# Moving the cached log-forget values into the first adaLN groups, and the decay chain into the first q tile, in a fused decode-step kernel

## The chip, the cores and the metric

The kernel runs on one core of one Trainium2 chip. The metric is device microseconds (us) of one execution of the whole program; lower is better. The kernel before took 1068.47 us (median of 3 runs, 1067.93 to 1070.03). The execution that was profiled took 1067.71 us; its trace spans 1066.1 us from the first to the last instruction, so 1.6 us lie around it. A core has five instruction queues that run side by side, each strictly in its own order: PE (matmul; its weight loads are listed as PEld), DVE (vector), ACT (scalar, activation functions and casts), POOL (GpSimd) and SP (used here only to issue DMAs). They wait for one another through semaphores.

## What is computed

One layer of a decoder trunk, in float32, for 512 prompt tokens and 8 single-token samples that share all weights (so 520 columns of activations), with D = 1024, 16 heads of 64, FFN width 2816:

```
m = silu(c) @ ada_w + ada_b      -> shift1, scale1, gate1, shift2, scale2, gate2
h = rms_norm(x) * (1 + scale1) + shift1
z = h @ w_in   -> rg_x | rg_gate | q | k | v | forget logits | gate A | gate B
branch A: width-4 causal conv -> RG-LRU -> * gelu(rg_gate) -> @ w_proj_a
branch B: forgetting attention, logit[t,s] = q_t.k_s/sqrt(dh) + sum_{s<j<=t} log f_j
          (samples attend to 1024 cached rows each, found through page_table)
x = x + gate1 * ((sigmoid(gA)*A + sigmoid(gB)*B) @ w_o)
x = x + gate2 * SwiGLU(rms_norm(x) * (1 + scale2) + shift2);  final rms_norm
```

For the samples, the sum of log f over the cached rows behind each row is needed: `cache_logf` is gathered by the page table (64 pages of 128 rows x 16 heads), and for every row the values after it are summed. RG-LRU needs `-8 * softplus(-lambda)` per channel (the decay), and the convolution needs, for the samples, the sum over the three stored inputs times their filter taps.

## The kernel before, in words

Activations lie feature-major: 8 tiles of 128 features x 520 tokens, worked on as two halves of 260. Every large product is made of three float32r products (high x high, low x high, high x low): each weight unit of 128 columns arrives by DMA (`wraw`, a ring of two 1 MB buffers), ACT casts its high part (`whi`, L210), DVE subtracts for the low part (`wlo`, L211), and PE runs 48 matmuls on it (`half_product`, L245). `begin` asks for weight chunks 22 us and for splits 11 us of PE time ahead. Evacuations are ACT's or DVE's.

**Start.** SP loads the parameters (L91), the constants up to column C_TRI (L92), x (L99) and the page table (L364, L366). ACT squares x, DVE adds, PE sums over features with an all-ones matmul (`ss`, L483, after feature tile 3 and after tile 7). Then `first_mod(0, ...)` (L410) runs the first half of adaLN's shift1 and scale1: eight groups `adaf` (L416), each behind its own 512 KB `araw` load (L413). ACT takes the two square roots (L488), DVE the reciprocals (L489) and eight products `xn` (L492). `first_mod_end` (L420) copies, transposes and adds, giving `n1amp`; `q_weights` (L449) splits the first q weights; `first_h` (L436) makes h for four feature tiles and PE starts the partial q products (`qp`, L467). The second half of adaLN is spread among these.

**q tiles.** A loop over i = 0..7 (L829 on) finishes q. In its turns stand: at i = 4 `past_load()` (POOL gathers 64 rows of 8 KB of log f, L371, into a buffer of the `wraw` ring) and the forget logits; at i = 6 their close, `decay()` (L599: Abs, Exp and a log1p of some twenty tiny DVE instructions on 128x8) and `past_conv()` (L807: eight products and a sum on DVE), and `past_turn(0)` (L380); at i = 7 `past_turn(1)`. `past_turn` transposes eight 64x128 blocks on PE into a bank (`lft`, L383), ACT copies it (`lk`, L385), and POOL makes the running sums over the pages behind (`after`: a memset, a copy and six dependent adds, L389 to L392). From i = 5 on, `tick` starts the sample attention: POOL loads cached key pages (L622) into a ring of seven 512 KB buffers (`pg`) that adaLN's `araw` tiles share, and DVE multiplies and sums them (L663/L664), which is what frees those buffers.

**First tiles of branch A.** The loop over i = 0, 2, 4, 6 (L980 on) runs two convolution products (`xr`), gate A (`ga`) and the RG-LRU gates (`gate`, L915, which need the split convolution `xch`/`xcl`, L278/L279), then gate B (`gb`) twice. `past_sums(0)` and `past_sums(1)` (L395) stand after the first and second `gb`: two 512-column float32 matmuls (`suf`, L398 and L399) and an ACT copy each. Then `ada_load(1, 6)` asks for the next adaLN weights (L296), the next `xr` runs, and `ada_piece(1, 6)` (L308) uses them. `suf` is first read by the softmax over the cached keys (L704).

**What sets the order.** The framework orders each engine's instructions by its own cost estimates; `with tc.issue_after(ins)` ties an instruction behind another of the same engine. `state["mm"]`, `state["act"]`, `state["last"]` hold the last tied PE, ACT and DVE instruction.

Of the kernel before, what the change touches and what calls it, by code (L numbers as in the profile page):

```python
# [64 lines left out]
def kernel(ctx, tc, xT, par, gates, b_f, cst, cse, own, cache_k, cache_v, cache_lf, pt,  # L65
# [13 lines left out]
    def slot(name, cols=NT, dt=F32, parts=128):  # L79
        return heap.tile([parts, cols], dt, name=name, tag="slot")  # L80
# [284 lines left out]
    idx = keep.tile([NS * NPAGE, 1], I32, name="idx")  # L365
    sp.dma_start(idx, pt.rearrange("a (b c) -> (a b) c", c=1))  # L366
    lfp = []

    def past_load():
# [10 lines left out]
    def past_turn(b):  # L380
        tp = bank(f"lft{b}")
        for n in range(8):
            pe.transpose(tp[:, 64 * n:64 * n + 64], lfp[0][:, 8 * b + n], ident[:64, :64])  # L383
        lk = slot("lk", 512)
        act.copy(lk, tp)  # L385
        after = slot("after", 512)
        lkv = lk.rearrange("p (a j) -> p j a", j=NPAGE)
        lav = after.rearrange("p (a j) -> p j a", j=NPAGE)
        pool.memset(lav[:, 7], 0.0)  # L389
        pool.tensor_copy(lav[:, 6], lkv[:, 7])  # L390
        for j in range(5, -1, -1):
            pool.tensor_tensor(lav[:, j], lav[:, j + 1], lkv[:, j + 1], ALU.add)  # L392
        lks.append((lk, after))

    def past_sums(b):  # L395
        lk, after = lks[b]
        sf = bank(f"suf{b}")
        pe.matmul(sf, lhsT=cs[:, C_TRI:C_TRI + 128], rhs=lk, start=True, stop=False)  # L398
        pe.matmul(sf, lhsT=ones, rhs=after, start=False, stop=True)  # L399
        t = slot("suf", 512)  # L400
        act.copy(t, sf)
        suf.append(t)


# [5 lines left out]
    def first_mod(fh, acc, kqs):  # L410
        for kq in kqs:
            raw = pgp.tile([128, 2, 512], F32, name="araw", tag="pg")
            sp.dma_start(raw, ada_w[kq * 128:kq * 128 + 128, :2048].rearrange("p (v c) -> p v c", v=2)  # L413
                         [:, :, 512 * fh:512 * fh + 512])
            for g in range(4):
                pe.matmul(acc[32 * g:32 * g + 32, :256], lhsT=silc[:, kq],  # L416
                          rhs=raw[:, g // 2, 256 * (g % 2):256 * (g % 2) + 256],
                          start=kq == 0, stop=kq == KT - 1, tile_position=(0, 32 * g))

    def first_mod_end(fh, acc):  # L420
        sb = slot("adas", 256)
        act.copy(sb, acc[:, :256])
        tp = bank(f"adaft{fh}")
        for b in range(2):
            pe.transpose(tp[:, b * 128:b * 128 + 128], sb[:, b * 128:b * 128 + 128], ident)
# [7 lines left out]
        dve.scalar_tensor_tensor(amp1[:, fs], mod[:, 1, fs], 1.0, prm[:, fs, P_N1:P_N1 + 1].to_broadcast([128, 4, 9]),  # L433
                                 ALU.add, ALU.mult)

    def first_h(f):  # L436
        t, hi, lo = slot("hr"), slot("hh", dt=F32R), slot("hl", dt=F32R)
        a_, b_ = amp1[:, f, 0:1], mod[:, 0, f, 0:1]
        act.activation(hi[:, :NP], xn[f][:, :NP], AF.Identity, scale=a_, bias=b_)
# [3 lines left out]
        act.copy(hi[:, NP:], t[:, NP:])  # L443
        dve.tensor_tensor(lo, t, hi.bitcast(F32), ALU.subtract)
        h.append((hi, lo))

# [2 lines left out]
    def q_weights(fh, raw, ko, i):  # L449
# [4 lines left out]
        src = raw[:, ko:ko + 4]  # L454
        for k in range(0, 4, 2 if (fh, i) == (0, 0) else 4):
            ks = slice(k, k + 2 if (fh, i) == (0, 0) else 4)
            state["act"] = act.copy(hi[:, ks], src[:, ks])
            state["last"] = dve.tensor_tensor(lo[:, ks], src[:, ks], hi[:, ks].bitcast(F32), ALU.subtract)
# [11 lines left out]
    def wraw():  # L470
        return wp.tile([128, KT, 256], F32, name="wraw", tag="wraw", bufs=2)

    ssq = [bank(f"ss1_{j}") for j in range(2)]
    for f in range(KT):
        t = slot("sq1")
        act.activation(t, x[f], AF.Square)
        if f % 4:
            dve.tensor_tensor(sq, sq, t, ALU.add)
        else:
            sq = t  # L480
        if f % 4 == 3:
            for j, (t0, t1) in enumerate(HALVES):
                pe.matmul(ssq[j][:, :HALF], lhsT=ones, rhs=sq[:, t0:t1], start=f == 3, stop=f == KT - 1)  # L483
    acc = [bank(f"adaf{fh}") for fh in range(2)]
    first_mod(0, acc[0], range(KT))
    r1 = slot("r1")
    for j, (t0, t1) in enumerate(HALVES):
        act.activation(r1[:, t0:t1], ssq[j][:, :HALF], AF.Sqrt, bias=eps, scale=1.0 / D)  # L488
        dve.reciprocal(r1[:, t0:t1], r1[:, t0:t1])  # L489
    for f in range(KT):  # L490
        t = slot("xn")
        dve.tensor_tensor(t, x[f], r1, ALU.mult)  # L492
# [29 lines left out]
    raw = wraw()  # L522
    q_weights(1, raw, 0, 4)
    load_chunks(0)
    sp.dma_start(cs[:, C_TRI:], cst[:, C_TRI:])


    def log1p(name, e, n, out):
# [300 lines left out]
    for i in range(KT):  # L829
# [150 lines left out]
    for i in range(0, KT, 2):  # L980
# [19 lines left out]
        if i < 6:  # L1000
# [586 lines left out]
```

## Time and profile before

| | us |
|---|---|
| median of 3 runs | 1068.47 |
| profiled execution | 1067.71 |
| its span | 1066.1 |
| PE busy | 1021.3 (96%) |
| DVE busy | 664.0 (62%) |
| ACT busy | 494.2 (46%) |
| POOL busy | 202.2 (19%) |

Timeline rows have: start, duration, engine, source line, operation, output<-inputs, how many were merged, and in brackets how long the engine had been idle before and what ended that wait. Rows of the windows view have: the stretch, its length, then for each engine the busy time and number of instructions, the granted PE clock (1.00 is full), the DMA engines' busy share, and GB/s. Rows of the waits view have: who waited, for whom, total us, times, longest us. "SPq" is the queue that issues DMAs; landing times are not in its durations.

### The profile page before, as it was taken

How to read it: one execution, taken by the hardware profiler on the slowest of the kernel's cores; microseconds unless marked ns; L12 is line 12 of the kernel's file. 1: busy time of each engine (PE TensorE's matmuls, PEld its weight loads, DVE VectorE, ACT ScalarE, POOL GpSimd, SP SyncE). 2: the span in 40 equal slices, each digit the busy share in tenths (PEclk: the TensorE clock that was granted, in tenths of full speed). 3: DMA queues.
4: the chain of work that ended last, by engine and by line, in shares of the span. 5: the costliest groups of instructions: out<-in, count | busy, mean ns of one | idle time of the engine just before them, and what ended most of it. 6: DMA issues, size and time to landing. Idle time of an engine off the chain costs nothing.

```text
span 1066.1 us, 21006 instructions
## 1 busy us (share of the span) xinstructions
PE 1021.3 (96%) x8210; PEld 948.1 (89%) x8210; DVE 664.0 (62%) x1166; ACT 494.2 (46%) x976; POOL 202.2 (19%) x348
## 2 busy tenths in 40 slices
PE   4999899999999999999999999999999999999994
PEld 2888779999998987888898989999999999999993
DVE  5447999988999986656765447733343333443363
ACT  4423565757782367767783235523212232123251
POOL 0224511112134234544400014100000000000022
PEclk9999899999999999999999999999999999999998
DMA  9898887778788998987746852232333332332212
GB/s 327 281 320 286 279 297 208 260 240 297 255 283 280 351 314 263 259 252 250 248 172 216 313 166 70 73 88 79 109 90 80 97 102 80 95 104 80 72 55 74
DMA packets 165285, 206.95 MB, mean 194 GB/s; under 512 B 9778, under 2 KB 126018, under 8 KB 165122
## 3 DMA queue, kind: packets, MB, share of 16 engines
q1 hardware_dynamic: 147746, 149.90, 45.6%
q0 software_dynamic: 13760, 49.29, 13.6%
q10 hardware_dynamic: 3680, 6.42, 1.6%
q8 instruction: 64, 1.05, 0.4%
q14 instruction: 35, 0.29, 0.1%
HBM read 192.49 MB, written 13.09 MB: 193 GB/s over the span
## 4 chain that ended last, share of the span: by engine, by line
PE 76%; DVE 9%; issue 4%; DMA 4%; ACT 4%; POOL 2%; POOLq 1%; SPq 0%; ACTq 0%; DVEq 0%
PE fiu L245 11%; PE fig L245 11%; PE fo L245 9%; PE pb L245 4%; PE k L245 4%; PE v L245 4%; PE pa L245 3%; PE gr L245 3%; PE gb L245 3%; PE ga L245 3%; PE xr L245 3%; PE wo L245 3%; PE pv L751 3%; DMA wraw<-in_w_in_dram 2%; PE qp L467 2%
## 5 line engine op out<-in xcount | busy, mean ns | idle before, releaser
L211 DVE TENSOR_TENSOR wlo<-wraw,whi 128x1024 fp32r<-128x1024 f32 (+1 forms) x131 | 160.7, 1227 | 159.3 <-ACT whi L210 153.2
L210 ACT CAST whi<-wraw 128x1024 fp32r<-128x1024 f32 (+1 forms) x131 | 136.7, 1043 | 242.7 <-PE fo L245 74.6
L337 POOL TENSOR_TENSOR ss<-ss,sq 128x260 f32<-128x260 f32 x18 | 13.6, 756 | 419.5 <-ACT sq L336 419.0
L245 PE MATMUL fiu<-h2h,wlo 128*128 128x260 f32 x320 | 90.5, 283 | 0.0
L245 PE MATMUL fig<-h2h,wlo 128*128 128x260 f32 x320 | 90.5, 283 | 0.0
L245 PE MATMUL fig<-h2l,whi 128*128 128x260 f32 x320 | 90.2, 282 | 0.0
L245 PE MATMUL fiu<-h2l,whi 128*128 128x260 f32 x320 | 90.2, 282 | 0.0
L245 PE MATMUL fig<-h2h,whi 128*128 128x260 f32 x320 | 90.2, 282 | 0.0
L245 PE MATMUL fiu<-h2h,whi 128*128 128x260 f32 x320 | 90.2, 282 | 0.0
L245 PE MATMUL fo<-ach,whi 128*128 128x260 f32 x292 | 82.8, 284 | 0.0
L245 PE MATMUL fo<-ach,wlo 128*128 128x260 f32 x292 | 82.5, 282 | 0.0
L245 PE MATMUL fo<-acl,whi 128*128 128x260 f32 x292 | 82.3, 282 | 0.0
L622 POOL DMA_DIRECT2D pg<-in_cache_k_dram x79 | 42.1, 533 | 115.8 <-DVE S L668 61.1
L245 PEld LDWEIGHTS fiu<-h2h,whi 128*128 128x128 f32 x320 | 60.2, 188 | 0.0
L245 PEld LDWEIGHTS fig<-h2h,whi 128*128 128x128 f32 x320 | 60.2, 188 | 0.0
L245 PEld LDWEIGHTS fig<-h2l,whi 128*128 128x128 f32 x320 | 60.2, 188 | 0.0
L245 PEld LDWEIGHTS fiu<-h2l,whi 128*128 128x128 f32 x320 | 60.2, 188 | 0.0
L245 PEld LDWEIGHTS fig<-h2h,wlo 128*128 128x128 f32 x320 | 60.1, 188 | 0.0
L245 PEld LDWEIGHTS fiu<-h2h,wlo 128*128 128x128 f32 x320 | 60.1, 188 | 0.0
L667 DVE TENSOR_TENSOR pg<-pg,qb 128x1024 f32<-128x1024 f32 x48 | 57.4, 1213 | 1.1 <-DMA pg<-in_cache_k_dram 1.0
L668 DVE TENSOR_REDUCE S<-pg 128x16 f32<-128x1024 f32 x48 | 57.2, 1207 | 0.0
L245 PEld LDWEIGHTS fo<-ach,wlo 128*128 128x128 f32 x292 | 55.1, 189 | 0.0
(388 smaller groups left out, 3445.6 us busy)
## 6 DMA issues: line engine op xcount, KB each, us to landing
araw<-in_ada_w_dram SPq DMA_DIRECT2D x48, 512.0 KB, 6.3
pg<-in_cache_k_dram POOLq DMA_DIRECT2D x47, 512.0 KB, 5.6
wraw<-in_w_fi_dram SPq DMA_DIRECT2D x44, 512.0 KB, 4.0
pg<-in_cache_v_dram SPq DMA_DIRECT2D x42, 512.0 KB, 4.9
wraw<-in_w_in_dram SPq DMA_DIRECT2D x34, 512.0 KB, 8.4
wraw<-in_w_in_dram SPq DMA_DIRECT2D x11, 1024.0 KB, 7.9
pg<-in_cache_v_dram POOLq DMA_DIRECT2D x22, 512.0 KB, 5.5
pg<-in_cache_k_dram POOLq DMA_DIRECT2D x32, 256.0 KB, 5.4
```

Of the source, the lines that this page charges most:

```text
L210: state["act"] = act.copy(hi[:, :k1 - k0], src)
L211: state["last"] = dve.tensor_tensor(lo[:, :k1 - k0], src, hi[:, :k1 - k0].bitcast(F32), ALU.subtract)
L245: state["mm"] = pe.matmul(out[:, :HALF], lhsT=wt[k], rhs=at, start=k == 0 and m == 0, stop=k == nk - 1 and m == 2)
L337: eng.tensor_tensor(acc[:, t0:t1], acc[:, t0:t1], q_, ALU.add)
L467: state["mm"] = pe.matmul(b[:, :HALF], lhsT=wt, rhs=at[:, t0:t1], start=k == 0 and m == 0, stop=k == 3 and m == 2)
L622: done.append(eng.dma_start(pg, cache[bass.ds(r, 1), :, c0:c1].rearrange("a p c -> (a p) c")))
L667: dve.tensor_tensor(pg, pg, q, ALU.mult)
L668: dve.tensor_reduce(S[r // 2][:, c:c + H], pg.rearrange("p (h d) -> p h d", d=DH), AX.X, ALU.add)
L751: pe.matmul(pv[0][32 * gq:32 * gq + 32, :], lhsT=pw[r][:, c:c + 32], rhs=pgs[gq // 2][:, 512 * hf:512 * hf + 512], start=j == 0, stop=j == ...
```

## The change

It moves work of the middle of the projection stage to earlier places and ties the order there:

- The page-table indices `idx` are SP's first load, and the constants are loaded up to C_S16 at once, so that the triangle matrix is there early.
- `past_load()` is called before x is squared. Its buffer is still one of the `wraw` ring's two, now the ring's first user instead of one in the middle.
- `past_turn` is cut in two: the transposes (both) run before feature tile 4 is squared, so between the two `ss` pairs on PE; the ACT copies and POOL sums (`past_after`) stand before and after the square roots.
- `past_sums(0)` is tied on PE between adaLN's fifth and sixth group, `past_sums(1)` between the seventh and the eighth; their ACT copies are tied behind the square roots.
- `first_mod_end(0)` is written ahead of the first q weights' split, and a few casts, `xn` and splits are tied in order.
- `decay()` and `past_conv()` move from turn 6 of the q loop to turn 0.

The diff, cut to its core:

```
+    idx = keep.tile([NS * NPAGE, 1], I32, name="idx")
+    sp.dma_start(idx, pt.rearrange("a (b c) -> (a b) c", c=1))
     sp.dma_start(prm, par)
-    sp.dma_start(cs[:, :C_TRI], cst[:, :C_TRI])
+    sp.dma_start(cs[:, :C_S16], cst[:, :C_S16])
...
             pe.transpose(tp[:, 64 * n:64 * n + 64], lfp[0][:, 8 * b + n], ident[:64, :64])
+        return tp
+
+    def past_after(tp):
         lk = slot("lk", 512)
         act.copy(lk, tp)
...
-        pe.matmul(sf, lhsT=cs[:, C_TRI:C_TRI + 128], rhs=lk, start=True, stop=False)
-        pe.matmul(sf, lhsT=ones, rhs=after, start=False, stop=True)
+        with tc.issue_after(state["mm"].ins):
+            pe.matmul(sf, lhsT=cs[:, C_TRI:C_TRI + 128], rhs=lk, start=True, stop=False)
+            state["mm"] = pe.matmul(sf, lhsT=ones, rhs=after, start=False, stop=True)
         t = slot("suf", 512)
-        act.copy(t, sf)
+        with tc.issue_after(state["act"].ins):
+            act.copy(t, sf)
...
-                pe.matmul(acc[32 * g:32 * g + 32, :256], lhsT=silc[:, kq],
+                with tc.issue_after(state["mm"].ins) if fh == 0 else nullcontext():
+                    mm = pe.matmul(acc[32 * g:32 * g + 32, :256], lhsT=silc[:, kq],
...
+    past_load()
     ssq = [bank(f"ss1_{j}") for j in range(2)]
     for f in range(KT):
+        if f == 4:
+            turned = [past_turn(b) for b in range(2)]
...
-    acc = [bank(f"adaf{fh}") for fh in range(2)]
-    first_mod(0, acc[0], range(KT))
+    past_after(turned[0])
     r1 = slot("r1")
     for j, (t0, t1) in enumerate(HALVES):
-        act.activation(r1[:, t0:t1], ssq[j][:, :HALF], AF.Sqrt, bias=eps, scale=1.0 / D)
+        state["act"] = act.activation(r1[:, t0:t1], ssq[j][:, :HALF], AF.Sqrt, bias=eps, scale=1.0 / D)
         dve.reciprocal(r1[:, t0:t1], r1[:, t0:t1])
+    past_after(turned[1])
+    acc = [bank(f"adaf{fh}") for fh in range(2)]
+    first_mod(0, acc[0], range(5))
+    past_sums(0)
+    first_mod(0, acc[0], range(5, 7))
+    past_sums(1)
+    first_mod(0, acc[0], range(7, KT))
...
+    first_mod_end(0, acc[0])
     q_weights(0, raw, 0, 0)
-    first_mod_end(0, acc[0])
...
+        if i == 0:
+            with tc.issue_after(state["last"].ins), tc.issue_after(state["act"].ins):
+                decay()
+                past_conv()
         if i == 4:
-            past_load()
             split_upto(1)
             close = forget_logits()
         if i == 6:
             close()
-            with tc.issue_after(state["last"].ins), tc.issue_after(state["act"].ins):
-                decay()
-                past_conv()
-            past_turn(0)
-        if i == 7:
-            past_turn(1)
...
             gate_b(i)
-            if i == 0:
-                past_sums(0)
             gate_b(i + 1)
             if i == 0:
-                past_sums(1)
                 ada_load(1, 6)
```

In the built order PE runs `ss` x2, 16 `lft`, `ss` x2, five `adaf` groups, `suf` (2), two groups, `suf` (2), one group, `adaft`. POOL runs the gather first, then `after` of half 0 (memset, copy, one add), memset and copy of half 1, and then eleven adds that alternate between the two halves. On DVE the twenty `lzc` instructions and the `cvp` products stand among the additions of the first q tiles; the log1p of the new forget logits (`fzc`, 128x65, 22 instructions), half of which stood much later, is now complete before the second `xcl`. On ACT one `lru_exp` moves ahead of the second half of the second gate B, with two more table loads. On SP the weight chunk after next is asked for earlier, since the ring no longer holds log f.

More of the change, by code (lines that the diff above doesn't have):

```diff
@@ L415, in first_mod @@
             for g in range(4):
-                pe.matmul(acc[32 * g:32 * g + 32, :256], lhsT=silc[:, kq],
-                          rhs=raw[:, g // 2, 256 * (g % 2):256 * (g % 2) + 256],
-                          start=kq == 0, stop=kq == KT - 1, tile_position=(0, 32 * g))
+                with tc.issue_after(state["mm"].ins) if fh == 0 else nullcontext():
+                    mm = pe.matmul(acc[32 * g:32 * g + 32, :256], lhsT=silc[:, kq],
+                                   rhs=raw[:, g // 2, 256 * (g % 2):256 * (g % 2) + 256],
+                                   start=kq == 0, stop=kq == KT - 1, tile_position=(0, 32 * g))
+            if fh == 0:
+                state["mm"] = mm
     def first_mod_end(fh, acc):
         sb = slot("adas", 256)
-        act.copy(sb, acc[:, :256])
+        state["act"] = act.copy(sb, acc[:, :256])
         tp = bank(f"adaft{fh}")
@@ L442, in first_h @@
         dve.tensor_scalar(t[:, :NP], xn[f][:, :NP], a_, b_, ALU.mult, ALU.add)
-        act.copy(hi[:, NP:], t[:, NP:])
+        last = act.copy(hi[:, NP:], t[:, NP:])
+        if f == 0:
+            state["act"] = last
         dve.tensor_tensor(lo, t, hi.bitcast(F32), ALU.subtract)
@@ L456, in q_weights @@
             ks = slice(k, k + 2 if (fh, i) == (0, 0) else 4)
-            state["act"] = act.copy(hi[:, ks], src[:, ks])
-            state["last"] = dve.tensor_tensor(lo[:, ks], src[:, ks], hi[:, ks].bitcast(F32), ALU.subtract)
+            with tc.issue_after(state["act"].ins) if fh == 0 and i < 4 else nullcontext():
+                state["act"] = act.copy(hi[:, ks], src[:, ks])
+            with tc.issue_after(state["last"].ins):
+                state["last"] = dve.tensor_tensor(lo[:, ks], src[:, ks], hi[:, ks].bitcast(F32), ALU.subtract)
         for n in range(2):
@@ L524 @@
     load_chunks(0)
-    sp.dma_start(cs[:, C_TRI:], cst[:, C_TRI:])
+    sp.dma_start(cs[:, C_S16:], cst[:, C_S16:])
     def log1p(name, e, n, out):
```

8 lines of the change are left out of this document (3 added, 5 removed).

## The prediction

> **What bounds the kernel now.** I read the page first, then the windows view cut at the ends of the stages, then the waits of PE.
>
> ```profile
> span 1066.1 us, 21006 instructions
> PE   4999899999999999999999999999999999999994
> ```
> ```profile
> 9.53:25.73 16.20, 10.73 (x75) 4.52 (x75) 12.17 (x18) 6.43 (x12) 1.19 (x3) 0.98 1.05 375
> 25.73:46.00 20.27, 20.27 (x159) 15.34 (x160) 6.93 (x13) 7.88 (x17) 2.77 (x6) 0.85 1.04 351
> 46.00:72.00 26.00, 26.00 (x216) 23.61 (x215) 15.84 (x29) 11.30 (x25) 5.74 (x14) 1.00 0.73 238
> ...
> 107.00:130.00 23.00, 17.91 (x127) 17.28 (x126) 21.36 (x41) 12.31 (x26) 11.87 (x20) 0.85 0.83 279
> 130.00:156.00 26.00, 23.67 (x168) 19.79 (x167) 26.00 (x27) 15.96 (x30) 4.77 (x9) 1.00 0.92 296
> 156.00:260.00 104.00, 104.00 (x854) 99.25 (x852) 97.28 (x135) 65.47 (x116) 15.84 (x30) 1.00 0.79 247
> ```
>
> PE bounds it: busy in nine tenths of nearly every slice. The windows show where it is not: the startup to 25.73, 107 to 130 (17.91 of 23.00, and a clock of 0.85), and 130 to 156 (23.67 of 26.00). From 156 to 260 PE is busy for 104.00 of 104.00. So a microsecond that PE saves or loses before 156 reaches the end of the kernel as long as the others keep up. In 107 to 156 DVE is nearly full (21.36 of 23.00, then 26.00 of 26.00): there it sets what PE waits for.
>
> ```profile
> PE gate L915 <- DVE xcl L279: 2.8, 1, 2.8
> ...
> PE ada L308 <- DMA araw<-in_ada_w_dram: 2.3, 2, 1.8
> ...
> PE gate L915 <- ACT xch L278: 1.3, 1, 1.3
> ...
> PE ga L245 <- DVE wlo L211: 0.9, 1, 0.9
> ```
>
> The change touches all of these: it takes PE work and DVE work out of the middle and puts PE, ACT and POOL work into the startup.
>
> **1. The startup, where work is added.**
>
> ```profile
> 6.48 0.57 SPq L366 DMA_DIRECT2D idx<-in_pt_dram  x1
> ```
> ```profile
> 12.61 2.10 PE L483 MATMUL ss<-sq,cs 128*128 128x260 f32 x4 [0.98 <-DVE sq L478]
> 14.39 3.41 DVE L489 RECIPROCAL r<-r 128x260 f32<-128x260 f32 x2 [1.84 <-ACT r L488]
> 17.84 4.97 DVE L492 TENSOR_TENSOR xn<-x,r 128x520 f32<-128x520 f32 x8
> 22.35 0.64 PE L416 MATMUL adaf<-araw,silc 128*32 128x256 f32 x8 [0.74 <-DMA araw<-in_ada_w_dram]
> 23.48 0.44 PE L425 MATMUL adaft<-cs,adas 128*128 128x128 f32 x2 [0.49 <-ACT adas L422]
> 25.73 0.58 PE L467 MATMUL qp<-hh,whi 128*128 128x260 f32 x1 [1.81 <-ACT hh L439]
> ```
> ```profile
> 107.19 1.21 DVE L211 TENSOR_TENSOR wlo<-wraw,whi 128x1024 fp32r<-128x1024 f32 x1
> ...
> 107.30 2.82 POOL L392 TENSOR_TENSOR after<-after,lk 128x64 f32<-128x64 f32 x2
> ...
> 110.61 0.93 POOL L392 TENSOR_TENSOR after<-after,lk 128x64 f32<-128x64 f32 x2
> ```
> ```profile
> 97.33 0.59 ACT L385 COPY lk<-lft 128x512 f32<-128x512 f32 x1
> 85.41 1.09 PE L383 MATMUL lft<-cs,lfp 64*128 64x64 f32 x8
> 86.43 1.07 PE L308 MATMUL ada<-araw,silc 128*32 128x512 f32 x8
> 135.50 1.02 PE L398 MATMUL suf<-lk,cs 128*128 128x512 f32 x2
> 136.36 1.02 PE L399 MATMUL suf<-after,cs 128*128 128x512 f32 x2
> 137.34 0.28 PE L245 MATMUL gb<-hh,wlo 128*128 128x260 f32 x1
> ```
>
> *Transfers.* `idx` now goes ahead of x on SP (0.57), and 512 KB of log f and some 64 KB more constants join a stream that already runs full (share 1.05, 375 GB/s): 1.6 us. Everything behind lands about 2 us later, the last `adaf` load too.
>
> *Roots.* The second `ss` pair ended at 14.71. Sixteen `lft` now stand ahead of it (eight take 1.02, from 85.41 to the next PE work at 86.43), partly beside x's later arrival. I put the end of the roots at 17.5. ACT then copies the second turned half (0.59) to 18.1, and POOL's own copy is done at about 18.5. Behind it POOL has eleven adds that alternate between the halves: the first half is complete with the tenth, the second with the eleventh.
>
> *POOL beside DVE.* Two adds took 0.93 when DVE did nothing with two operands (110.61), and 2.82 beside `wlo` and the page product behind it (107.30): 0.47 or 1.41 each, that is one 1.21 DVE instruction plus 0.2. In the startup the eight `xn` are such instructions, 0.62 each (4.97 / 8), and start when the reciprocals end: 17.80 before, about 20.4 after. So four adds are free, and the other six to the tenth take 0.62 + 0.2 to 0.62 + 0.47; I take 0.9. The first half is ready at 18.5 + 4 x 0.47 + 6 x 0.9 = 25.8, the second at 26.7; with no alternation the tenth ends at 23.2.
>
> The Trainium skill, "SBUF — State Buffer", section "SBUF: two separate sides", says that a DVE instruction with two SBUF inputs and a GpSimd instruction reading SBUF exclude each other, one blocked for the whole of the other. The rows at 107.30 and 110.61 agree. By that rule the alternation is certain; without it the sum below would come out as the first rival.
>
> *Who waits.* The `ones` half of `past_sums(0)` needs the first half and is tied ahead of groups six to eight, so the whole rest of `adaf` queues behind it on PE, and behind that n1amp, h and q. That rest is 0.86 (half of 135.50 to 137.22, the two matmuls of one `past_sums`) + 0.96 (three groups at 0.32, from 22.35) + 1.72 = 3.5 at full clock, 7.1 at half, which is what PE had behind its wait in the middle (part 4). I take 6.0, nearer to the half clock. `adaf` ends at 31.8 instead of 22.99. From there to the first `qp` it was 25.73 - 22.99 = 2.74, kept: q starts at 34.5, raw +8.8.
>
> *Given back.* The clock was 0.85 over 25.73 to 46: 0.15 x 20.27 = 3.0 us lost to a half clock. If PE is warm when q starts later, most of this is not lost again; I take 2.3. **Startup: +6.5.** Low end: 23.2 + 3.5 + 2.74 - 25.73 = 3.7, less 2.7: +1. High end: 25.8 + 7.1 + 2.74 - 25.73 = 9.9, less 0.9: +9.
>
> **2. What leaves the middle on PE.** Two times `lft`, 1.02 each: **-2.0**. Two times `suf`, 1.72 each (135.50 to 137.22, `gb` follows without a gap): **-3.4**. PE's neighbours stand close on both sides, so they count whole.
>
> **3. The waits at the gates.**
>
> ```profile
> 82.14 1.23 DVE L663 TENSOR_TENSOR pg<-pg,qb 128x1024 f32<-128x1024 f32 x1 [4.36 <-DMA pg<-in_cache_k_dram]
> 89.92 1.22 DVE L211 TENSOR_TENSOR wlo<-wraw,whi 128x1024 fp32r<-128x1024 f32 x1 [2.92 <-ACT whi L210]
> ...
> 111.31 1.31 DVE L663 TENSOR_TENSOR pg<-pg,qb 128x1024 f32<-128x1024 f32 x1 [1.16 <-DMA pg<-in_cache_k_dram]
> ```
> ```profile
> L536 DVE TENSOR_TENSOR lzc<-lzc,lzb 128x8 f32<-128x8 f32 x7 | 2.2, 308 | 0.0
> L537 DVE TENSOR_SCALAR lzc<-lzc 128x8 f32<-128x8 f32 x7 | 2.0, 292 | 0.0
> ```
> ```profile
> 124.73 0.23 DVE L536 TENSOR_TENSOR fzc<-fzc,fzb 128x65 f32<-128x65 f32 x1
> ```
>
> The decay chain and the convolution sums stood on DVE ahead of `xcl`. The two groups above are 4.2 us for 14 of its instructions; with the others, less overlap, I put the block at 4.9. In the built order the remaining twelve `fzc` (0.23, with what lies between them some 0.25 each, 3.0) move in ahead of the second `xcl`. DVE's work there falls by only 1.9. The rest must come from DVE's idle time: 4.36 at 82.14 (first key page; its load is now issued ahead of `qb`), 2.92 at 89.92 (the cast waited for a weight chunk that was asked for late, since log f sat in that ring), 1.16 at 111.31. If all goes, DVE is 1.9 + 8.4 = 10.3 earlier; if only the last, 3.1. The waits sum to 0.94 + 1.31 + 2.83 = 5.1 (0.9, 1.3 and 2.8 in the rows above). PE itself arrives 2.0 earlier there (part 2), so all of it goes if DVE comes 7.1 earlier, and only 1.1 of it with 3.1. I take the 10.3: **-5.1**.
>
> *Where it goes.* The chain's instructions land in 46 to 72, where DVE is busy 15.84 of 26.00; cost 0, and up to 4.9 if q's additions there wait.
>
> **4. The clock behind them.**
>
> ```profile
> 119.03 0.58 PE L915 MATMUL gate<-xcl,gws 128*128 128x260 f32 x1 [2.83 <-DVE xcl L279]
> ...
> 121.36 0.42 PE L245 MATMUL ga<-hh,whi 128*128 128x260 f32 x1
> ...
> 124.08 0.28 PE L245 MATMUL ga<-hh,wlo 128*128 128x260 f32 x1
> ```
> After the gate wait the same matmul takes 0.42 where it takes 0.28 at 124.08. The granted clock of this stage is 0.85: 0.15 x 23.00 = 3.5 us of clock lost, which at half speed is 6.9 us, up to about 124. Some 2 us of these lie in the wait itself, where nothing is lost; from 119.03 on it is 4.9 us at half speed, estimated at 4.9 x 0.45 = **-2.2** when the wait goes.
>
> The Trainium skill, "TensorE: Matmul & The Clock Gate", section "Part 1: The HAM clock gate (the "warmup" mystery)", has a free-running window of about 3.4 us: an idle window halves the clock, a busy one restores it. The rows agree; if in the startup the window falls badly, q starts at half clock once more, and the sum would be 2.3 higher, 1065.8.
>
> **5. The wait that comes next.**
>
> ```profile
> 146.23 2.34 DVE L664 TENSOR_REDUCE S<-pg 128x16 f32<-128x1024 f32 x2
> ...
> 152.42 1.05 PE L308 MATMUL ada<-araw,silc 128*32 128x512 f32 x4 [1.79 <-DMA araw<-in_ada_w_dram]
> ```
> ```profile
> 145.50 1.28 ACT L924 ACT_TABLE_LOAD   x1
> ```
>
> `ada_piece(1, 6)` waits for loads that take buffers of the key-page ring, free when DVE has summed the pages: the first of the sums at 146.23 ends at 147.4, and the second load lands about 6.6 later: PE starts on it at 154.0 (152.42 + 1.05 + the other 0.5 of the 2.3 that the waits view has). PE comes 2.0 + 3.4 + 5.1 + 2.2 = 12.7 sooner and would want that load at 139.0 (150.6 + 1.05 - 12.7). With DVE 10.3 earlier it lands at 143.7 and the wait is 4.7, against 2.3: +2.4; I take **+2.0**. Bounds: -2.3 if it lands in time, +9.6 with DVE only 3.1 earlier. The two extra table loads on ACT (1.28 each) lie in 130 to 156 with ACT busy 15.96 of 26.00: 0, or 2.6 without that cover.
>
> **The sum.** 1067.71 (profiled; span 1066.1 and 1.6 around it) + 6.5 - 2.0 - 3.4 - 5.1 - 2.2 + 2.0 = 1063.5. The profiled run lies 0.8 under the median of 1068.47, within its spread.
>
> **Rivals.** *A, the startup is nearly free:* no alternation, the sums ready at 23; +1 instead of +6.5, **1058.0**. For it: POOL is idle there (1.19 of 16.20). Against: the row at 107.30. *B, slower:* the key-page sums stay as late as they were, because DVE's 4.36 and 2.92 us of idle time are page and weight transfers in a stretch with DMA at 0.86 to 0.92 that are not sooner for being asked sooner. Then 6.5 - 12.7 + 9.6 + 2.2 (the clock falls again behind an idle time of 12 us) = +5.6: **1073.3**. It decides where the sums at 146, the startup apart, come less than about 4.4 us earlier (6.5 - 4.4 = 2.1, the bound of no change), and it holds wherever PE does its waiting ahead of them, at the gates or at `ada`. *C, the startup at its high end* and the clock cold at q: +9 and 1 to 2 us of cover lost, **1067**, no change. *That the change doesn't do what it says:* the built order has `lft`, `suf` and the decay at their new places, so what is left of this is that they wait there, which is case C.
>
> **How the numbers follow.** Forecast 0.45, A 0.2, B 0.2, C 0.15. Range 1057 to 1071: it holds A and C, and leaves out most of B and a startup that costs nothing. A measurement tells about 0.2%, 2.1 us. Faster: forecast mostly and A, 0.62; same: C and the forecast's upper edge, 0.16; slower: B and a little of C, 0.22.
>
> **What would show it.** First `qp` at 34.5 rather than 25.73, with PE idle ahead of the `suf` that waits for POOL `after`; single adds near 0.9 beside `xn`; the clock at 1.00 soon after; no `gate` wait for `xcl` or `xch` over 0.5 us and no 0.50 clock near 107 to 113; the `ada` wait at 3 to 6 us. It is wrong if q starts before 30 or after 37, if `xcl` is still waited for, or if PE has a new hole behind 156.

## The result, and the profile after

The changed kernel takes 1073.54 us (median of 11 runs, 1068.49 to 1076.58), the kernel before 1068.47 us (11 runs, 1067.23 to 1071.49). The ratio is 1.0038, with a 95% interval of 1.0024 to 1.0052: some 4 us slower (the medians lie 5.1 apart). The forecast was 1063.5, with a range of 1057 to 1071. The profiled execution's span is 1071.9 us, 5.8 more than before.

The page of the changed kernel, and its windows cut at the same times as before:

```profile
span 1071.9 us, 21014 instructions
...
PE   3999979999999999999999999999999999999994
```
```profile
9.53:25.73 16.20, 10.02 (x66) 5.81 (x66) 8.74 (x11) 6.37 (x10) 5.67 (x13) 1.00 1.04 356
25.73:46.00 20.27, 17.29 (x113) 9.23 (x117) 12.13 (x20) 7.85 (x15) 7.33 (x12) 0.92 0.99 336
...
107.00:130.00 23.00, 22.19 (x180) 21.55 (x180) 20.84 (x41) 11.97 (x27) 7.51 (x14) 1.00 0.86 274
130.00:156.00 26.00, 18.90 (x150) 17.34 (x150) 26.00 (x27) 17.12 (x28) 3.73 (x7) 0.90 0.87 266
156.00:260.00 104.00, 103.15 (x838) 97.10 (x833) 96.98 (x125) 63.51 (x113) 16.44 (x32) 0.99 0.78 241
```

The hole has moved. In 107 to 130 PE is now busy for 22.19 of 23.00 (17.91 before), in 130 to 156 only for 18.90 of 26.00 (23.67 before), with DVE still busy for all 26.00. The waits of PE say the same:

```profile
PE ada L310 <- DMA araw<-in_ada_w_dram: 7.1, 1, 7.1
PE suf L403 <- POOL after L395: 2.7, 1, 2.7
...
PE gate L933 <- DVE xcl L281: 0.6, 1, 0.6
PE gate L933 <- ACT xch L280: 0.2, 1, 0.2
```

The gate waits (4.1 us before, and the 0.9 us for `wlo`) are down to 0.8, the wait at `ada` has grown from 2.3 to 7.1, and there is a new one for POOL's sums in the startup. In the startup the timeline of the changed kernel has:

```profile
13.98 2.10 PE L498 MATMUL ss<-sq,cs 128*128 128x260 f32 x4 [13.98 <-DMA x<-in_xT_dram]
16.02 2.03 PE L383 MATMUL lft<-cs,lfp 64*128 64x64 f32 x16
...
17.98 2.10 PE L498 MATMUL ss<-sq,cs 128*128 128x260 f32 x4
...
19.76 3.42 DVE L503 RECIPROCAL r<-r 128x260 f32<-128x260 f32 x2 [3.03 <-ACT r L502]
...
21.39 6.94 POOL L395 TENSOR_TENSOR after<-after,lk 128x64 f32<-128x64 f32 x11
...
23.21 6.28 DVE L513 TENSOR_TENSOR xn<-x,r 128x520 f32<-128x520 f32 x8
...
26.71 1.12 PE L403 MATMUL suf<-after,cs 128*128 128x512 f32 x2 [2.71 <-POOL after L395]
...
32.32 0.64 PE L422 MATMUL adaf<-araw,silc 128*32 128x256 f32 x8
...
35.26 0.39 PE L479 MATMUL qp<-hh,whi 128*128 128x260 f32 x1 [1.36 <-ACT hh L447]
```

x lands later (the first `ss` at 13.98 instead of 9.53): its fourth tile, asked for at 4.00, landed at 12.54, just behind log f, which POOL had asked for at 3.45 and which landed at 12.36. The roots end 5.4 us later, the POOL sums end at 28.33, `adaf` ends at 32.96 and the first `qp` starts at 35.26. Where the lag goes from there is seen by setting the start of the same PE work side by side in the two timelines:

| PE work | before | after | lag |
|---|---|---|---|
| first qp | 25.73 | 35.26 | +9.5 |
| first q | 52.19 | 60.81 | +8.6 |
| first xr (two lft less) | 95.52 | 102.05 | +6.5 |
| second ga | 121.36 | 122.32 | +1.0 |
| first gb | 129.73 | 129.78 | 0.0 |
| third xr (two suf less) | 144.30 | 141.27 | -3.0 |
| gr behind ada(1,6) | 154.99 | 157.37 | +2.4 |
| second ga of the next pair | 182.06 | 185.79 | +3.7 |
| ada in wo's stage | 569.04 | 574.36 | +5.3 |
| end of the span | 1066.1 | 1071.9 | +5.8 |

Nearly all that was to be saved on PE was saved: from 8.6 behind at the first q it comes to 3.0 ahead at the third `xr`, 11.6 us of the forecast 12.7. Then it waits at `ada` until it is 2.4 us behind. The rows of that place, and of the start of the key-page work on DVE:

```profile
87.74 1.23 DVE L684 TENSOR_TENSOR pg<-pg,qb 128x1024 f32<-128x1024 f32 x1 [6.27 <-DMA qb<-qtd]
...
99.48 1.23 DVE L684 TENSOR_TENSOR pg<-pg,qb 128x1024 f32<-128x1024 f32 x1 [2.37 <-DMA pg<-in_cache_k_dram]
...
103.91 1.23 DVE L684 TENSOR_TENSOR pg<-pg,qb 128x1024 f32<-128x1024 f32 x1 [0.82 <-DMA qb<-qtd]
...
116.59 0.75 DVE L912 SCALAR_TENSOR_TENSOR xc<-xr,prm,xc 128x509 f32<-128x509 f32 x1 [1.61 <-ACT xc L906]
...
149.46 1.21 DVE L685 TENSOR_REDUCE S<-pg 128x16 f32<-128x1024 f32 x1
...
151.19 1.21 DVE L685 TENSOR_REDUCE S<-pg 128x16 f32<-128x1024 f32 x1
...
154.27 3.17 PE L310 MATMUL ada<-araw,silc 128*32 128x512 f32 x8 [7.10 <-DMA araw<-in_ada_w_dram]
...
157.37 0.55 PE L247 MATMUL gr<-hh,whi 128*128 128x260 f32 x1
```

The first page product starts at 87.74 (82.14 before) and waits for `qb`, the q of the samples, not for a page. The two loads for `ada(1,6)` are issued as the fourteenth and the fifteenth of the page sums end, at 147.27 and 150.66 (144.05 and 147.44 before), so 3.2 us later. The sixteenth, which below is called the last sum, ends at 152.40 (148.57 before). Behind the wait the first matmul takes 0.55: the clock is down again, as it was behind the gates before.

### The profile page after: what moved, and what is told of

Its sections match the earlier page's. It is cut to its first block, busy times and chain, and to the rows that moved or that the text cites. A ratio compares the mean times of both kernels' runs of the same rounds, so it can differ in the third digit from the quotient of the medians.

```text
span 1071.9 us, 21014 instructions
## 1 busy us (share of the span) xinstructions
PE 1022.0 (95%) x8210; PEld 946.6 (88%) x8210; DVE 663.5 (62%) x1166; ACT 496.2 (46%) x978; POOL 199.7 (19%) x348
## 4 chain that ended last, share of the span: by engine, by line
PE 76%; DVE 9%; issue 4%; DMA 4%; ACT 4%; POOL 2%; SPq 0%; POOLq 0%; ACTq 0%; DVEq 0%
PE fiu L247 11%; PE fig L247 11%; PE fo L247 9%; PE pb L247 4%; PE k L247 4%; PE pa L247 3%; PE gr L247 3%; PE v L247 3%; PE gb L247 3%; PE ga L247 3%; PE xr L247 3%; PE wo L247 3%; PE pv L772 3%; PE qp L479 2%; DVE wlo L213 2%
```

## The experiments

Theory T: the late start delays q, q delays `qb`, and with it all key-page work on DVE; the sums release the buffers of adaLN's last loads, so PE's savings end in the wait at `ada`. Theory R: the new order on DVE makes the sums late whatever the start does. Ratios are to the kernel before, with 95% intervals.

### The decay chain alone

```
 (kernel before)
+        if i == 0:
+            decay(); past_conv()
         if i == 6:
             close()
-            decay(); past_conv()
```

> The kernel before, with only the decay chain and the convolution sums moved to the first q tile; the startup and the log f work stay as they were. Theory T (the startup's 9.5 us delay the whole key-page path, and that path sets when adaLN's last weights can be loaded): the startup costs nothing here, DVE loses 4.9 us of work ahead of the gates, so the gate waits (5.1 us in sum before) shrink to under 2.5, the wait at ada L308 grows from 2.3 to 3 to 5, and PE passes it 0 to 4 us earlier: 1064.5 to 1068. Theory R (the new order on DVE, with the fzc chain ahead, makes the key-page sums late whatever the startup does): PE passes ada at 155 or later: 1069 to 1073.

1070.7 us, ratio 1.0015 (1.0000 to 1.0029). Nothing is gained at all: T's numbers failed. R's came (PE passes `ada` at 155.1), but not by R's reason: it is idle time of DVE that grows, from 5.0 to 11.6 us by the windows shown with the next run. The gate waits did not shrink, and the timeline shows why:

```profile
PE gate L916 <- ACT xch L278: 6.1, 1, 6.1
```
```profile
107.66 1.23 DVE L663 TENSOR_TENSOR pg<-pg,qb 128x1024 f32<-128x1024 f32 x1 [2.83 <-DMA pg<-in_cache_k_dram]
...
110.52 1.23 DVE L663 TENSOR_TENSOR pg<-pg,qb 128x1024 f32<-128x1024 f32 x1 [1.64 <-DMA pg<-in_cache_k_dram]
...
117.23 0.62 ACT L278 CAST xch<-xc 128x520 fp32r<-128x520 f32 x1 [9.25 <-DVE xc L895]
```

DVE, relieved of the chain (forecast at 4.9 us; in the windows shown with the next run its busy time falls by 3.5), waits 2.83 and 1.64 us for key pages instead, and the convolution's `xc`, which `xch` needs, stands behind those products in DVE's order. So in the kernel before the chain seems to have filled time in which no page was there.

### past_sums back behind gate B

```
 (changed kernel)
-    first_mod(0, acc[0], range(5)); past_sums(0)
-    first_mod(0, acc[0], range(5, 7)); past_sums(1)
-    first_mod(0, acc[0], range(7, KT))
+    first_mod(0, acc[0], range(KT))
...
             gate_b(i)
+            if i == 0: past_sums(0)
             gate_b(i + 1)
             if i == 0:
+                past_sums(1)
                 ada_load(1, 6)
```

> The changed kernel with the two past_sums put back behind gate B, all else as changed (log f still gathered beside x, turned and summed in the startup). T: adaf no longer queues behind POOL's sums, the first qp starts at 28 to 30 instead of 35.3, and the suf matmuls (3.4 us) fall into time that PE waits at ada anyway: 1065 to 1069. R: the start gains but ada still ends near 157: 1072 to 1076.

1066.11 us, ratio 0.9964 (0.9947 to 0.9981): faster than the kernel before, and some 7 us faster than the changed one. First `qp` at 30.92 (28 to 30 expected), sums done at 148.33, `gr` at 154.84. The time is T's, the way there only in part. The first q is 3.2 us sooner than in the changed kernel and the first `qb` landed 2.9 sooner (84.70 for 87.62), yet the first page product starts at 87.55 (87.74): now it waits for a key page, 4.30 us. The 4.1 us won at the sums were won behind it. (The profiled execution took 1069.02 us, the longest of its nine, so it cannot show what was gained on the kernel before.) To see what the key-page path did, the windows view is cut from the first page product to the end of the last sum; the third figure of time in a row is DVE's busy time (behind the length, PE and PEld). Before, after, decay alone, and this kernel:

```profile
82.10:148.55 66.45, 61.36 (x459) 55.85 (x458) 61.42 (x101) 30.74 (x61) 26.74 (x49) 0.95 0.83 276
```
```profile
87.70:152.40 64.70, 58.66 (x476) 55.01 (x474) 59.27 (x81) 35.37 (x67) 18.69 (x36) 0.99 0.90 287
```
```profile
80.50:150.05 69.55, 62.49 (x468) 57.10 (x467) 57.91 (x75) 30.06 (x61) 26.85 (x49) 0.93 0.81 273
```
```profile
87.50:148.30 60.80, 59.25 (x459) 53.41 (x457) 57.33 (x75) 30.39 (x62) 17.86 (x33) 1.00 0.91 299
```

Before: 66.45 long, DVE busy 61.42, idle 5.0. After: 64.70, 59.27, idle 5.4: the work fell by 2.15 (forecast 1.9), the idle time did not fall. Decay alone: work 57.91, idle 11.6. This kernel: 57.33 and idle 3.5, so against the changed one 1.9 less of either.

### ada(1,6) later on PE

```
 (changed kernel)
-                ada_piece(1, 6)
-                ada_load(1, 7)
             both(lru_root, i - 2)
             gelu(i - 2)
+            if i == 2:
+                ada_piece(1, 6)
+                ada_load(1, 7)
```

> The changed kernel with ada_piece(1,6) and the load for (1,7) written behind the first gelu product (6 us of PE work) instead of ahead of it. T: the 7.1 us wait is covered down to 0 to 2 us and no cold clock follows: 1067 to 1070. R: DVE is late for everything there, so PE waits for weight splits or gates instead, the sum of its waits between 107 and 200 stays above 7: 1072 to 1076.

1075.52 us, ratio 1.0048 (1.0032 to 1.0065). T's number failed and R's came: the wait is not covered.

```profile
PE ada L310 <- DMA araw<-in_ada_w_dram: 9.4, 4, 4.4
```

Four waits at `ada` of 9.4 us in sum take the place of one of 7.1. But this moved the load for (1,7) as well, so a second run moved only the matmuls:

```
 (changed kernel)
-                ada_piece(1, 6)
                 ada_load(1, 7)
             both(lru_root, i - 2)
             gelu(i - 2)
+            if i == 2:
+                ada_piece(1, 6)
```

> The changed kernel with only the matmuls of ada_piece(1,6) behind the first gelu product; both loads stay where they were. If the 7.1 us wait is a matter of PE's order alone, it is covered and the time falls to 1067 to 1070. If the key-page sums on DVE are the floor of the whole stage, PE waits for something else of DVE's a few us later (gates, weight splits, the next ada) and the time stays within 1072 to 1076.

1073.42 us, ratio 1.0040 (1.0025 to 1.0054): as the changed kernel. The wait at `ada` falls to 2.4, the gate waits grow from 0.8 to 1.8, and two others of DVE's, the sample softmax, come a stage later:

```profile
PE ga L247 <- DVE pw L742: 3.8, 1, 3.8
...
PE lgt L730 <- DVE mk L727: 1.2, 1, 1.2
```

So the wait is not a matter of where `ada` stands on PE. DVE, full there, is the floor.

### x first, and the turning behind the second ss

```
 (as with past_sums behind gate B)
-    sp.dma_start(idx, ...)          # ahead of x
+    load_x(); sp.dma_start(idx, ...); sp.dma_start(cs[:, C_TRI:C_S16], ...)
-        if f == 4:
-            turned = [past_turn(b) for b in range(2)]
...
+    turned = [past_turn(b) for b in range(2)]
     past_after(turned[0])
     r1 = slot("r1")
```

> As the run with past_sums back behind gate B, and x is loaded ahead of the page table, the gather and the further constants, and the turning stands behind the second ss. T: x lands as before the change, the roots end near 15.3 instead of 20.6, the first qp starts at 25.7 to 28; the decay's 4.9 us on DVE are still gone from the middle: 1062 to 1067. R: 1070 to 1074.

1075.85 us, ratio 1.0051 (1.0034 to 1.0069): a miss, by an edit of mine. Log f lands late behind x, and the first `lk` copy still stood ahead of the roots on ACT:

```profile
20.98 2.04 PE L384 MATMUL lft<-cs,lfp 64*128 64x64 f32 x16 [6.40 <-DMA lfp<-in_cache_lf_dram,idx]
...
24.07 0.85 ACT L502 ACTIVATE r<-ss,eps 128x260 f32<-128x260 f32 x2
```

The roots run at 24.07, the first `qp` at 35.31. It is of use all the same: with a first `qp` as late as the changed kernel's, and a first q 1.8 us later, the first product comes at 92.17, the sums end at 155.55 and `gr` starts at 161.52. The second try kept log f out of the way of roots and `adaf`:

```
 (as with past_sums behind gate B)
     load_x(); sp.dma_start(idx, ...)
...
     first_mod_end(0, acc[0])
     q_weights(0, raw, 0, 0)
+    turned = [past_turn(b) for b in range(2)]   # tied behind adaft
     for f in range(4):
         first_h(f)
+    past_after(turned[0]); past_after(turned[1])
```

> As the run with past_sums back behind gate B, but x is loaded ahead of the page table and the gather, the turning stands on PE between adaft and the first qp (where PE waited 1.8 us for h before), and the copies and POOL sums behind the first four h. Nothing of log f then stands ahead of the roots or of adaf. T (each us by which the first qp is late is paid at the end): first qp at 26 to 29 instead of 30.5 to 31, and 1 to 4 us less than that run: 1062 to 1066. If the start were not what decides: the same as that run, 1066 to 1068.

1065.06 us, ratio 0.9967 (0.9955 to 0.9980), by its median as fast as with `past_sums` alone moved back, by its profile ahead of it (sums done at 145.96, `gr` at 151.41). The first `qp` came at 29.63, later than expected: `adaf` itself waited 5.0 us for its loads (2.2 before), which log f's 512 KB push back.

### past_sums in the q tiles

```
 (changed kernel, first_mod(0, ...) in one piece)
+        if i == 1:
+            past_sums(0)
+            past_sums(1)
```

> The changed kernel with both past_sums in turn 1 of the q tiles, where PE is never idle, instead of among adaf. T: the startup wait goes as in the run with past_sums behind gate B, but their 3.4 us are now paid in q, ahead of the key pages, instead of lying in a wait of PE: 0 to 4 us slower than that run, 1066 to 1070, and still 4 to 7 faster than the changed kernel. If the startup wait were not the cost: 1072 to 1076.

1071.28 us, ratio 1.0031 (1.0018 to 1.0044). The startup wait is gone here too (first `qp` at 30.96), and yet most of the loss is there, more than T's 1066 to 1070. PE was 5.0 us ahead of the kernel before at the third `xr`, and waited:

```profile
153.23 3.20 PE L310 MATMUL ada<-araw,silc 128*32 128x512 f32 x8 [8.08 <-DMA araw<-in_ada_w_dram]
```

So `past_sums` cost PE nothing where it stood before: it lay ahead of a wait. Moved into q it puts PE 3.5 us further behind there (4.1 behind the kernel before at the first q, 7.5 at the first `ada`). That did not reach the first product, though, which is at 86.75, 0.8 sooner than with `past_sums` behind gate B. The loss at the sums lies behind it. From first product to last sum it is 63.65 us with DVE busy 59.08, 1.75 more work than with `past_sums` behind gate B: as in the changed kernel, the built order has two q additions, a product of the RG-LRU (`th`) and the forget logits' small work on DVE ahead of the last sum. That order came with the place of `past_sums`; it was not tried by itself.

### log f alone

```
 (as with past_sums behind gate B)
-        if i == 0:  decay(); past_conv()
         if i == 6:
             close()
+            decay(); past_conv()
```

> As the run with past_sums back behind gate B, and the decay chain and the convolution sums also back in turn 6: what stays of the change is that log f is gathered beside x, turned and summed on POOL in the startup. Theory P (in the middle it was POOL's queue, where the sums of log f and their waits stood among the key-page loads, that set the pace; DVE's decay chain only filled gaps in which DVE waited for pages): about as fast as with the decay moved, 1065 to 1068. Theory V (DVE's work sets the pace, and both parts are needed together): the 4.9 us come back, 1069 to 1072.

1067.85 us, ratio 0.9996 (0.9980 to 1.0011). In the profile the sums end at 148.18 and `gr` starts at 154.75, as with the decay moved (148.33 and 154.84): P. But the first product came 1.8 us sooner (85.78), and from there to the last sum it is 62.4 us for 60.8, so the two profiles do not differ in the decay alone. By the times the decay's place is worth 0.3%, with intervals that just meet. This run did not decide it; two more took POOL's sums out of the kernel before, once without and once with the decay moved:

```
 (kernel before, and the same with the decay in turn 0)
-        after = slot("after", 512)
-        pool.memset(...); pool.tensor_copy(...); six pool.tensor_tensor(...)
+        after = lk
```

> The kernel before with nothing moved, only the running sums of log f on POOL left out (suf is formed from lk in their place). P: the key pages come sooner, but DVE still has the decay chain: 0 to 4 us less than before, 1065 to 1069, and less gained than by the same step with the decay chain moved. If POOL's sums were harmless: 1068 to 1069.5.

> The kernel before with the decay chain and the convolution sums in the first q tile (as in the first run of this series), and with the running sums of log f on POOL left out (suf is formed from lk in their place, so the sums over the pages behind are missing from the computation). Theory P (the POOL sums and their waits among the key-page loads set the pace): DVE's idle time between its first page product and the last sum ahead of ada(1,6), 11.6 us there, falls to 4 to 6, the wait for xch (6.1) falls under 3: 3 to 6 us less than that run, 1064 to 1068. If pages are late for another reason: as that run, 1069 to 1072.

Without the decay moved 1066.89 us, ratio 0.9993 (0.9977 to 1.0009); with it 1067.42 us, ratio 0.9983 (0.9969 to 0.9997). The sums end at 146.41 and 146.77, 2.2 and 3.3 us sooner than in the kernels with POOL's sums (148.57 and 150.07). Counted from the first product (81.02 and 82.16, before 82.14 and 80.58) the path is 1.0 and 4.9 us shorter. So POOL's sums among the page loads did cost the page path something, and moving the decay gains nothing there either way: DVE's idle time in the path is 6.3 without and 7.1 with it moved, where P expected 4 to 6 for the latter.

Without the decay moved, what POOL's sums cost was not idle time but DVE's work. The windows of log f alone, and of the kernel before without POOL's sums:

```profile
85.70:148.15 62.45, 60.30 (x465) 54.21 (x464) 58.80 (x101) 32.00 (x64) 19.82 (x35) 1.00 0.88 291
```
```profile
81.00:146.40 65.40, 61.48 (x476) 55.76 (x475) 59.07 (x101) 32.62 (x66) 16.97 (x33) 1.00 0.89 291
```

DVE runs the same 101 instructions in both and in the kernel before, and is busy for 58.80, 59.07 and, beside POOL's sums, 61.42 us. The tiny `lzc` instructions of the decay chain show it most: beside POOL's sums their median is 0.29 to 0.30 us, without 0.15 to 0.17.

### A late start alone

```
 (kernel before)
-        for b in range(2):
+        for b in list(range(2)) * (24 if fh == 0 else 1):
             pe.transpose(tp[:, b * 128:b * 128 + 128], ...)
```

> The kernel before, with the two adaft transposes repeated 24 times (the same result each time), so that n1amp, h and q start some 5 to 9 us later and nothing else is moved. T (key pages and PE both hang on q, so nothing downstream absorbs a late start): the time rises by 0.7 to 1 of what the first qp is late, and the ada wait and the gate waits stay about as they are. Rival: the middle has 9 to 10 us of waits and cold clock on PE that take a late start up, because the key-page path has its own pace: it rises by less than a third of it.

1070.48 us, ratio 1.0014 (0.9997 to 1.0032).

```profile
30.87 0.39 PE L467 MATMUL qp<-hh,whi 128*128 128x260 f32 x1 [1.43 <-ACT hh L439]
...
84.23 1.23 DVE L663 TENSOR_TENSOR pg<-pg,qb 128x1024 f32<-128x1024 f32 x1 [8.22 <-DMA qb<-qtd]
```

The first `qp` is 5.1 late, the first q 3.2 (a warm clock gives 2.0 back), the first page product 2.1, the sums 2.3, the time 1.5 (-0.3 to 3.4). So in this profile a late start is passed on to the page path (2.3 of 3.2) and, by the ratio, 1.5 to the time: about half of the 3.2, and of the 5.1 less than T said and within the rival's third. The interval also holds no loss at all. PE's waits in the middle (gates, `wlo`, `ada`) fell from 7.4 to 5.6 and the clock of 107 to 130 rose from 0.85 to 0.93, so they took up a part, as the rival has it, while the sums moved as T has it. The wait of the first product is for `qb`, as in the changed kernel.

### A buffer of its own for log f

```
 (as x first, turning late)
-    heap = ... bufs=60          t = wp.tile(..., tag="wraw", bufs=2)
+    heap = ... bufs=56          t = keep.tile(...)
     for f in range(4):
         first_h(f)
+    past_load()                 # tied behind h's last POOL instruction
...
+        if i in (1, 2):
+            past_after(past_turn(i - 1))
```

> A version made to keep both gains: decay chain early, log f in a buffer of its own (the heap has 56 instead of 60 slots for it), gathered behind the first four h, turned and summed in q turns 1 and 2, ahead of the first key-page load on POOL, past_sums behind gate B. T: first qp at 25.5 to 26.5 as before the change, lft costs 2.1 us in q, POOL is free for the key pages: 1061 to 1065. If four heap slots are missed, or the start is not what decides: 1066 to 1070.

1073.0 us, ratio 1.0035 (1.0017 to 1.0052). The first half of T's expectation held, the time came out above both of its ranges:

```profile
25.67 0.59 PE L481 MATMUL qp<-hh,whi 128*128 128x260 f32 x1 [1.82 <-ACT hh L449]
```
```profile
PE ptt L1173 <- DVE ksB L1073: 1.4, 1, 1.4
PE ptt L1173 <- ACT ph L1177: 0.7, 1, 0.7
```

The sums end at 144.67 and `gr` starts at 149.85, 5.1 us ahead of the kernel before. From about 390 on, in the attention of the prompt, new waits in which heap tiles take part use that up and more: by 396 PE is 0.7 behind the kernel before, at 1033 4.0. That they come of the four missing slots was not shown.

### All runs side by side

First page product, end of the last sum, DVE's idle time between them, and start of the first `gr`, each from the profiled execution:

| kernel | first product | last sum | idle | gr | ratio |
|---|---|---|---|---|---|
| before | 82.14 | 148.57 | 5.0 | 154.99 | 1 |
| changed | 87.74 | 152.40 | 5.4 | 157.37 | 1.0038 |
| decay alone | 80.58 | 150.07 | 11.6 | 155.13 | 1.0015 |
| sums behind gate B | 87.55 | 148.33 | 3.5 | 154.84 | 0.9964 |
| the same, decay back | 85.78 | 148.18 | 3.7 | 154.75 | 0.9996 |
| x first, lk ahead of the roots | 92.17 | 155.55 | 5.1 | 161.52 | 1.0051 |
| x first, turning late | 85.82 | 145.96 | 4.1 | 151.41 | 0.9967 |
| sums in q | 86.75 | 150.38 | 4.6 | 156.36 | 1.0031 |
| before, late start | 84.23 | 150.86 | 3.9 | 155.60 | 1.0014 |
| before, no POOL sums | 81.02 | 146.41 | 6.3 | 152.82 | 0.9993 |
| decay alone, no POOL sums | 82.16 | 146.77 | 7.1 | 153.97 | 0.9983 |
| log f in its own buffer | 84.24 | 144.67 | 3.2 | 149.85 | 1.0035 |

In every row the two loads for `ada(1,6)` are issued within 0.1 us of the ends of the fourteenth and fifteenth sum, and `gr` starts 4.7 to 7.2 us behind the sixteenth, whatever PE did before: that is the floor. From `gr` to the end of the span it is 911.1 us (before) to 914.5 (changed) in all rows but the last, where it is 920.2. The ratio orders the rows roughly, not exactly, by `gr`, and the last row not at all. The two runs with `ada(1,6)` later on PE are left out, since there `gr` stands ahead of it.

## Why the prediction was wrong

The forecast was 4.2 us under the profiled execution before, and the profiled span came out 5.8 over. Of these 10.0 us the startup is 2.1 (8.6 for 6.5), PE's savings up to `ada` 1.1 (11.6 for 12.7), `ada` with the clock behind it 3.4 (5.4 for 2.0), and what came behind `ada` 3.4 (2.4 to 5.8, no term of the sum).

*The startup (+6.5).* The mechanism was right and the place too: the `suf` that waits for POOL, `adaf` queued behind it, first `qp` at 35.26 for 34.5. Two sizes were off. Beside `xn` the adds took turns with it, an `xn` every 0.83 us, near the 0.9 taken, but they began at 21.39 and not at 18.5, since x itself came 4.5 us later, not 2. The first half was ready at 26.65 all the same, 0.9 later than forecast: five adds had begun before `xn` did, and it was complete with the ninth, not the tenth (`suf` starts at 26.71). And by the first q PE had won back 0.9, not 2.3, though the granted clock read 1.00 from the first `qp` to the first q (0.89 before). The term was +8.6.

*lft and suf (-2.0, -3.4).* -2.1 (8.6 to 6.5) and -3.1 (0.0 to -3.0). Right as lengths of PE work.

*The gate waits and the clock (-5.1, -2.2).* -6.5 together. The sum was near, the cause was not: moving the decay by itself left gate waits of 7.0. In the changed kernel the first `xcl` ended at 120.96, 2.0 us later than before (118.97), and PE came to the gates 6.5 later, so the same lateness that was booked as a cost in the startup is what made the waits go. (Of the forget logits' chain not all came ahead of the second `xcl`: three `fzc` and `fl` stand behind it, at 127.86 to 128.58.) It can be had without: with a buffer of its own for log f PE came 2.4 us late, the first `xcl` ended at 115.12, and no gate wait is left.

*The step that failed* is "The rest must come from DVE's idle time: 4.36 at 82.14 ... 2.92 at 89.92 ... 1.16 at 111.31 ... I take the 10.3", and with it the +2.0 at `ada`. Counted from the first q, which is 8.6 late, the last sum came 4.8 us sooner and not 10.3 (the fifteenth 5.4). DVE was relieved of its 2.15 us of work. Of the idle time only 2.6 went: 3.0 ahead of the first product, which is 5.6 late, less 0.4 more within the path (5.4 for 5.0). Counted so, the key page was there sooner, as forecast (its loads, issued ahead of `qb`, had landed by 84.95, before by 81.95), but now the product waits for `qb` (6.27 in place of the 4.36), and `qb` hangs on q, which the startup had delayed. The 2.92 and the 1.16 went, and 2.37 for a page, 0.82 for `qb` and 1.61 for `xc` took their place. PE arrived 3.0 us ahead, and left `ada` 2.4 behind: 5.4 where +2.0 was booked.

*Rival B* came nearest in kind: the sums stay the bound at `ada`, wherever PE does its waiting. It had a chance of 0.2, and the range left most of it out. But by its own line, sums less than 4.4 us earlier with the startup taken off, it was missed: 4.8 to 5.4. That its price (+5.6) is near the +5.1 of the medians is luck: it had 11.8 for `ada` and the clock, where 5.4 was measured, 6.5 for the startup, where it was 8.6, and nothing for the 3.4 behind `ada`. What the argument lacked was in the trace of before: POOL's queue stood 2.4 us until q had gone its way through DRAM (`qtd`) before it could ask for `qb`, so the page path could not leave a late start behind.

*Behind `ada`* the lag grows from 2.4 to 3.7 by 186 (among it a wait of 0.8 for the sample softmax, again DVE's) and to 5.3 at 569, which the last section explains for this execution. No step of the prediction had either.

*Still open:* how much of the loss is the late start and how much the other order on DVE and POOL that came with the places of `past_sums` (1.9 us more DVE work ahead of the last sum than with them behind gate B). Of a late start alone, at the sums it passed on 2.3 of 3.2 us; the same share of the changed kernel's 8.6 is 6.2, less the 2.15 of lighter DVE work 4.1, and 3.8 was measured. That fits the start as the whole cause of the late sums, but two runs don't. With `past_sums` behind gate B the first q was 3.2 sooner and the first product was not, and the whole gain at the sums lay within the path. And `past_sums` in q, with a first `qp` 4.3 us sooner than the changed kernel's, was only 2.0 sooner at the sums and 0.7% of the time away from `past_sums` behind gate B. The start alone explains neither. What is shown is that it was the place of `past_sums`: put back by itself, it took away the whole loss.

## What to carry to other kernels

Before counting a removed wait as a gain, find what will be waited for next, and follow that back to its own start: here the buffers came free by sums, the sums began with q, and q began with the very startup that the change burdened. Work that stands on PE just ahead of a wait for another engine costs nothing where it is; moved to the front of the program it delays everyone. And idle time of a full engine is a gain only if what it waited for also comes sooner.

## What the hardware showed beside this

A wait of PE can cost 1.5 us more in one execution than in another of the same length. `pb` has two waits, 0.8 and 1.0 us, in both kernels (they end at 564.4 and 566.0 before, 568.2 and 569.8 after). Behind them the windows are, before and after:

```profile
570.00:580.00 10.00, 10.00 (x87) 9.97 (x84) 5.77 (x9) 2.50 (x4) 0.00 (x0) 1.00 0.88 300
```
```profile
570.00:580.00 10.00, 10.00 (x70) 9.03 (x70) 3.90 (x12) 2.07 (x7) 0.00 (x0) 0.83 0.34 104
```

The granted clock there is 1.00 before (also in 560 to 570) and 0.83 after (0.50 in 572 to 574): 0.17 x 10 = 1.7 us of clock, and the lag grows by 1.5. With `past_sums` behind gate B it reads 0.83 in 560 to 570, 1.00 in 570 to 580. So the same two waits halved the clock for a while in two of these executions and not in the third. What decides it, and whether some of the scatter of these runs (1063 to 1069 us for that kernel) is of this kind, was not shown.

POOL's adds lengthened DVE's products too, which the prediction had not counted: the eight `xn` took 6.28 us for 4.97. Where each had an add beside it, the `xn` started 0.83 us apart, less than 0.62 and the 0.41 of an add alone (the one at 18.24) together. The Trainium skill, "SBUF — State Buffer", section "SBUF: two separate sides", has such a pair exclude one another for the whole instruction; the turns agree with that, the sum of the times does not quite: some 0.2 us of a pair passed side by side.
